# A band mask folded into a one-hot matmul, and the last tile's two stores on one queue, in a two-layer encoder

## The chip, the cores and the metric

One core of one Trainium2 chip runs the whole program. The metric is the device time of one execution in microseconds (us), as the median of several runs; less is better. The core has five engines that run side by side and wait for each other by semaphores: TensorE (PE in the profile; PEld is its weight load), VectorE (DVE), ScalarE (ACT), GpSimd (POOL) and SyncE (SP), which issues nearly all DMA transfers of this kernel.

## The reference

Two encoder layers of 1024 tokens by 1024 features. Layer 0 has windowed attention with a learned sink and a relative-position bias (A), dense attention with rotary positions (B) and cross-attention into a memory (X); layer 1 has differential attention with the same bias (C), and X. The change concerns the bias of A and C:

```python
def rel_bias_lookup(table, rel):            # table: 32 buckets x 6 heads
    return jnp.moveaxis(table[t5_bucket(rel)], -1, 0).astype(jnp.float32)

# A: blocks of 128 queries, each against 384 keys
rel = c - BLOCK - a                          # a: 0..127, c: 0..383
bias = rel_bias_lookup(table, rel)
valid = (jnp.abs(rel) <= WINDOW) & ...       # WINDOW = 128
logits = jnp.where(valid, logits + bias, NEG_INF)
p = softmax(concatenate([logits, sink_col]))[..., :-1]

# C: every query against all 1024 keys, bias added, no band
p = softmax(s + rel_bias_lookup(table, rel))
```

After each layer the output is projected and added to the residual; at the end a last RMSNorm is taken of every row.

## The kernel before

**Work and order.** Activations are kept transposed, features on partitions, as a high and a low float32r part, so that a projection tile (`proj_jobs`, L329) is 24 matmuls of 128x512 for each half of the tokens. Attention goes in steps of 128 queries, and projections ("jobs") are cut into pieces that are pulled between the steps to fill PE. `run_steps` writes out the order by hand: in step i it emits the scores of step i, the transposes of an earlier step, the product with V of a still earlier one, and job pieces between them. Tile then places the instructions on the engines; each engine, and the SP queue of transfers too, works strictly in its own order.

**The bias.** `tab` holds the bias table, negated, because the kernel takes all scores negative. One matmul of `tab` with a one-hot matrix `oh` (32 buckets by 512 relative positions) gives `vp`, one row for each head; it goes over `vs` to `vec_d` in HBM. `skew(h)` writes row h 128 times into `skew_d`, so that `skew_src(h)`, read with a row step of 511, gives a 128x384 tile in which each row is shifted by one against the row above. Layer 1 loads that tile as part of `toep` (`load_toep`). Layer 0 loads it into `ab` (`a_bias`, two buffers, one load for each of the six A heads, while the head before is at work), and POOL then adds `mask`, a 128x384 tile from HBM with 1e30 outside the band (L1152). The scores of an A step, `sa`, are read by DVE's L1184, which adds `ab` and writes `e`.

**The loop around it in layer 0.** A step's scores become exponentials in a tile `e` (three buffers; ACT's L1110 for B, L1188 for A). DVE takes the reciprocal of the row sums (`rz`, L1113 or L1192), POOL multiplies `e` by it (L1114 for B, L1198 for A), SP copies `e` to `er` (`word_copy`, L175), PE transposes `er` (`te`, `ta`). The buffer `e` is free for the third step after it when that copy has landed. POOL also takes the head outputs times the gate (`gy`, L473, from DVE's `yt`, L472) and the low parts of weights (`wl`, L243).

**The tail.** The last of the 16 row tiles is scaled in two parts, 384 columns on ACT (L1349) and 640 on DVE (L1350). Each is stored by a transfer of its own: the 384 columns by ACT's queue (L1352), the 640 by SP's. It is the only transfer that ACT issues.

Of the kernel before, what the change touches and what calls it, by code (L numbers as in the profile page):

```python
# [12 lines left out]
F32 = mybir.dt.float32  # L13
F32R = mybir.dt.float32r
AF = mybir.ActivationFunctionType
ALU = mybir.AluOpType
# [23 lines left out]
XB = 0  # L40
ABLAG = 3
PRE = ((((2, 3, 4, 5), 4), ((6,), 6), ((7,), 6)), (((2, 3), 6), ((4,), 6)))
SPARE = 24
LATE = 22

TILES = (
# [109 lines left out]
def encoder_kernel(ctx, tc, A):  # L156
# [15 lines left out]
    def dma(out, in_, eng=None):  # L172
        if out.dtype == F32R and in_.dtype == F32R:
            out, in_ = out.bitcast(F32), in_.bitcast(F32)
        (eng or nc.sync).dma_start(out=out, in_=in_)  # L175
# [14 lines left out]
    misc = const.tile([P, 8], F32, name="misc")  # L190
    gq, nlam, gs, ls, le = (misc[:, a:b] for a, b in ((0, 1), (1, 2), (2, 3), (3, 5), (5, 7)))
    nsink = const.tile([P, 6], F32, name="nsink")
    tab = const.tile([32, 6], F32, name="tab")
    edge = pool(ctx, "edge", "right").tile([P, 120], F32, name="edge")
    spare = const.tile([P, SPARE], F32, name="spare")
    for t in (spare, edge):
# [12 lines left out]
    memT_d = [dr.tile([P, KT, MEM], F32R, name="memT%d" % i) for i in range(2)]  # L209
    wo_d = [[[dr.tile([P, 8, 512], F32R, name="wo%d%d%s" % (l, nh, c)) for c in "hl"] for nh in range(2)]  # L210
            for l in range(2)]
    vec_d = dr.tile([6, 512], F32, name="vec_d")
    skew_d = dr.tile([6, P, 512], F32, name="skew_d")

    nc.gpsimd.memset(sm.tile([P, 16], F32, tag="pad", name="pad", bufs=1), 0.0)

# [182 lines left out]
    def sg(M, name="sg", dt=F32R):  # L399
        return M.pl.tile([P, 512], dt, tag="sg", name=name, bufs=M.cfg["sg"])  # L400
# [633 lines left out]

    dma(tab, A["rel_bias"])
    nc.vector.tensor_scalar(out=tab, in0=tab, scalar1=-1.0, scalar2=None, op0=ALU.mult)
    oh = sg(M, "oh", F32)[:32, :]
    dma(oh, A["onehot"])  # L1040
    vp = ps_t("vp")
    nc.tensor.matmul(vp[0:6, :], tab, oh, start=True, stop=True)
    vs = sg(M, "vs", F32)[:6, :]
    nc.vector.tensor_copy(vs, vp[0:6, :])
    dma(vec_d, vs)

    def skew(h):
        dma(skew_d[h], bass.AP(vec_d.tensor, vec_d.offset + h * 512, [[0, P], [1, 512]]))
# [15 lines left out]
    def skew_src(h):  # L1064
        return bass.AP(skew_d.tensor, skew_d.offset + h * P * 512 + 127, [[511, P], [1, 384]])
# [74 lines left out]
    def open_ab():  # L1140
        top_stack.close()
        ab = pool(top_stack, "ab", "right")
        mask = ab.tile([P, 384], F32, name="mask")
        dma(mask, A["mask"])
        abias["mask"], abias["pool"] = mask, ab
        M.xpool, M.xbufs = ab, XB

    def a_bias(h):
        mask = abias["mask"]
        t = abias["pool"].tile([P, 384], F32, tag="ab", name="ab", bufs=2)  # L1150
        dma(t, skew_src(h))
        nc.gpsimd.tensor_tensor(out=t, in0=t, in1=mask, op=ALU.add)  # L1152
        abias[h] = t

    if True:
# [96 lines left out]

    def hooks0(i):
        if 2 <= i < 8:
            skew(i - 2)
        if i < 0:
            wout_hook(0, jobs, "g2", r1)

# [6 lines left out]
    def out_proj(l, hT_next, stack, ahead=None):  # L1265
        op = pool(stack, "op%d" % l, "right" if l == 0 else "left")
        gb = bcast_row(op, A["odd_norm"][0] if l == 0 else A["final_norm"], "gb")
        while len(wout) < 16:
            wout[len(wout)] = load_wout(l, len(wout), r1 if l == 0 else r2)
        src = x_d if l == 0 else x1sc  # L1270
        ne = EARLY[l]
        pre = {t: k for ts, k in PRE[l] for t in ts if "pre%d" % t in jobs.done}

        def xres(t):
            xr = op.tile([P, D], F32, tag="xr", name="xr", bufs=2)
            dma(xr, (xpsc[l] if t in pre else src)[t * P:(t + 1) * P, :])
            return xr

        def pieces(i):
            if i == 2:  # L1280
                p = [(ps_a("po")[:, 0:512], c, 512) for c in (0, 512)]
                return p, p
            if i < TT - 1:
                S2 = ps_s("po")
                return [(S2[:, 0:512], 0, 512), (S2[:, 512:1024], 512, 512)], [(S2, 0, 1024)]
            p = [(ps_a("po")[:, 0:512], 0, 512)]
            for c, n in ((512, 512),) if l == 0 else ((512, 256), (768, 256)):
                p.append(((ps_a if c == 512 else ps_t)("po")[:, 0:n], c, n))
            return p, p

        mms = []

        def mm(ps_, ch, ks, first):
            for acc, c, n in ps_:
                for k in ks:
                    for _ in y_mm(acc, ch, c // 512, k, k == first, k == 7, slice(c % 512, c % 512 + n)):
                        mms.append(lastmm[0])

        def turn():
            while pend and len(mms) >= pend[0][2]:  # L1300
                xs, t, d = pend.pop(0)
                transpose_tile(xs, hT_next, t, mms[d - 1])

        def chunk(t):
            return y_chunk(l, t, range(pre.get(t, 0), 8))

        order = ORD[l]
        pend, due = [], [0]
        chs = [chunk(t) for t in order[:2]]
        accs = {}  # L1310
        for i in range(2):
            t = order[i]
            accs[i] = pieces(i)
            mm(accs[i][0], chs[i], range(pre.get(t, 0), ne), pre.get(t, 0))
        xrs = [xres(t) for t in order[:2]]
        for i, t in enumerate(order):
            xr = xrs[i]
            mps, eps = accs[i] if i < 2 else pieces(i)
            mm(mps, chs[i], range(ne if i < 2 else pre.get(t, 0), 8), pre.get(t, 0))
            if i + 2 < TT:  # L1320
                chs.append(chunk(order[i + 2]))
                xrs.append(xres(order[i + 2]))
            turn()
            rows = slice(t * P, (t + 1) * P)
            x1 = op.tile([P, D], F32, tag="x1", name="x1", bufs=2)
            xs = op.tile([P, D], F32, tag="xs", name="xs", bufs=2)
            ss = stat("z4", 4)
            tail = l == 1 and i == TT - 1
            for j, (acc, c, n) in enumerate(eps):
                h = slice(c, c + n)  # L1330
                nc.vector.tensor_tensor(out=x1[:, h], in0=acc, in1=xr[:, h], op=ALU.add)
                nc.scalar.activation((xr if tail or l == 0 else xs)[:, h], x1[:, h], AF.Square,
                                     accum_out=ss[:, j:j + 1])
                if tail:
                    nc.vector.tensor_tensor(out=xs[:, h], in0=x1[:, h], in1=gb[:, h], op=ALU.mult)
                elif l == 0:
                    nc.gpsimd.tensor_tensor(out=xs[:, h], in0=x1[:, h], in1=gb[:, h], op=ALU.mult)
                if l == 0:
                    dma(x1sc[rows, h], x1[:, h])

            v = stat("v")
            nc.vector.tensor_scalar(out=v, in0=ss[:, 0:1], scalar1=1.0 / D, scalar2=EPS, op0=ALU.mult, op1=ALU.add)
            for j in range(1, len(eps)):
                nc.vector.scalar_tensor_tensor(out=v, in0=ss[:, j:j + 1], scalar=1.0 / D, in1=v,
                                               op0=ALU.mult, op1=ALU.add)
            r = stat("r")
            rstd_from(r, v, 1)
            if tail:
                nc.scalar.activation(xs[:, 0:384], xs[:, 0:384], AF.Identity, scale=r)  # L1349
                nc.vector.tensor_scalar(out=xs[:, 384:1024], in0=xs[:, 384:1024], scalar1=r, scalar2=None,  # L1350
                                        op0=ALU.mult)
                nc.scalar.dma_start(out=out_d[rows, 0:384], in_=xs[:, 0:384])  # L1352
                dma(out_d[rows, 384:1024], xs[:, 384:1024])
            elif l == 0:
                nc.scalar.activation(xs, xs, AF.Identity, scale=r)
            else:
                for _, c, n in eps:
                    h = slice(c, c + n)
                    nc.vector.scalar_tensor_tensor(out=xs[:, h], in0=x1[:, h], scalar=r, in1=gb[:, h],
                                                   op0=ALU.mult, op1=ALU.mult)  # L1360
                    dma(out_d[rows, h], xs[:, h])
            if l == 0:
                due[0] = max(len(mms) + LATE, due[0] + 18)
                pend.append((xs, t, due[0]))
        while pend:
            next(ahead)
            mms.extend([lastmm[0]] * 8)
            turn()
# [267 lines left out]
def _constants():  # L1636
# [14 lines left out]
    large = 8 + (np.log(nf / np.float32(8)) / np.float32(math.log(16.0)) * np.float32(8)).astype(np.int32)  # L1651
    large = np.minimum(large, 15)
    b = np.where(rel > 0, 16, 0) + np.where(n < 8, n, large)
    onehot = (np.arange(32)[:, None] == b[None, :]).astype(np.float32)
    r = np.arange(384)[None, :] - 128 - np.arange(128)[:, None]
    mask = np.where(np.abs(r) <= 128, 0.0, 1e30).astype(np.float32)
    return dict(cosT=cosT, sinT=sinT, onehot=onehot, mask=mask)


# [14 lines left out]
```

## Time and profile before

| | |
|---|---|
| median of 3 runs | 1227.74 us (1226.81 to 1227.98) |
| profiled execution, its own time | 1230.69 us |
| its span, first to last instruction | 1228.9 us |
| PE busy | 1196.5 us, 97% of the span |
| DVE, ACT, POOL busy | 65%, 54%, 36% |
| mean granted TensorE clock | 0.996 |

The span is what the trace covers; 1.8 us of the execution's own time lie outside it. Busy shares are means over stages: what an engine's work is worth is read at the place where someone waits for it. In the rows below, a time in brackets is how long the engine sat idle before the row, and behind the arrow is what ended that.

### The profile page before, as it was taken

The page shows a single profiled execution, that of the slowest core. Times are in us where ns is not written, and L with a number is a line of the kernel's source. Part 1 is how long each engine was busy: PE and PEld are TensorE (multiplying, and loading weights), DVE is VectorE, ACT ScalarE, POOL GpSimd, SP SyncE. Part 2 cuts the span into 40 slices and gives each one's busy share as a digit, 9 for nine tenths or more (in the row PEclk, how much of TensorE's full clock was granted, in tenths as well). Part 3 has the DMA queues.
Part 4 walks back from the last instruction along what each step waited for, and adds up shares of the span by engine and source line. Part 5 has one row for each costly group of instructions (what it writes and reads, how often), then busy time and mean ns, then how long its engine had stood idle before and what let it go on. Part 6 is the DMA issues. An engine that isn't in the chain of part 4 may idle for free.

```text
span 1228.9 us, 19560 instructions
## 1 busy us (share of the span) xinstructions
PE 1196.5 (97%) x6614; PEld 988.4 (80%) x6614; DVE 801.1 (65%) x1495; ACT 663.1 (54%) x1477; POOL 436.3 (36%) x414
## 2 busy tenths in 40 slices
PE   6999999999999999999999999999999999999997
PEld 5788888888888777888888777777787777777886
DVE  5547665377778878635365866766767767667544
ACT  6248754366667766636157744555545454445332
POOL 5023365366665455437112222333143231301100
PEclk9999999999999999999999999999999999999999
DMA  6664445545465565457645445355363452468354
GB/s 257 200 194 147 163 172 163 166 160 207 163 233 209 208 227 191 151 196 237 186 158 156 153 146 164 121 183 163 124 187 125 153 171 105 149 212 285 121 192 155
DMA packets 114304, 216.70 MB, mean 176 GB/s; under 512 B 13302, under 2 KB 47478, under 8 KB 114204
## 3 DMA queue, kind: packets, MB, share of 16 engines
q1 hardware_dynamic: 114060, 215.25, 52.5%
q8 instruction: 53, 0.87, 0.3%
q14 instruction: 47, 0.39, 0.1%
q10 hardware_dynamic: 144, 0.20, 0.0%
HBM read 87.71 MB, written 39.86 MB: 104 GB/s over the span
## 4 chain that ended last, share of the span: by engine, by line
PE 47%; DVE 2%; DMA 1%; issue 1%; ACT 1%; POOL 0%; POOLq 0%; SPq 0%; DVEq 0%; ACTq 0%
PE acc L329 24%; PE po L702 5%; PE oc L1545 3%; PE sc L1505 3%; PE te L580 3%; PE sc L1514 2%; PE pre L702 2%; PE oc L1547 2%; DMA wr<-in_w_in 1%; PE ssqc L1563 1%; PE ox L656 0%; PE rbcc L1576 0%; PE tv L439 0%; PE sx L543 0%; DVE e L1520 0%
## 5 line engine op out<-in xcount | busy, mean ns | idle before, releaser
L329 PE MATMUL acc<-h,wh 128*128 128x512 f32 x1536 | 499.5, 398 | 1.6 <-DVE h L351 0.8
L329 PEld LDWEIGHTS acc<-h,wh 128*128 128x128 f32 x1536 | 282.4, 188 | 65.7 <-issue 7.9
L329 PE MATMUL acc<-h,wl 128*128 128x512 f32 x768 | 303.8, 396 | 1.5 <-POOL wl L243 1.2
L243 POOL TENSOR_TENSOR wl<-wr,wh 128x512 fp32r<-128x512 f32 x94 | 124.8, 1329 | 286.3 <-DVE wh L241 155.0
L1523 ACT ACTIVATE e<-e,mn 128x1024 f32<-128x1024 f32 x96 | 110.0, 1148 | 117.0 <-DVE mn L1520 116.9
L329 PEld LDWEIGHTS acc<-h,wl 128*128 128x128 f32 x768 | 144.3, 188 | 34.9 <-issue 4.4
L1114 POOL TENSOR_TENSOR e<-e,rz 128x1024 f32<-128x1024 f32 x48 | 91.6, 1910 | 84.2 <-DVE rz L1113 57.8
L1520 DVE CUSTOM_DVE_ANT_0 e<-sc,toep 128x1024 f32<-128x1024 f32 x96 | 113.5, 1218 | 8.0 <-PE sc L1514 7.3
L580 PEld LDWEIGHTS te<-identr,er 128*128 128x128 f32 x896 | 92.2, 143 | 18.8 <-PE sa L543 2.2
L580 PE MATMUL te<-identr,er 128*128 128x128 f32 x896 | 99.9, 246 | 4.3 <-DVE O L1578 1.4
L348 DVE TENSOR_TENSOR PT<-te,PT 128x512 fp32r<-128x512 f32 x112 | 74.3, 687 | 42.8 <-ACT PT L347 39.2
L241 DVE CAST wh<-wr 128x512 fp32r<-128x512 f32 x112 | 58.2, 522 | 42.9 <-PE acc L329 17.3
L348 DVE TENSOR_TENSOR PTl<-te,PTh 128x512 fp32r<-128x512 f32 x112 | 74.0, 684 | 9.4 <-ACT PTh L347 8.9
L1545 PE MATMUL oc<-PT,v 128*128 128x512 f32 x192 | 69.8, 403 | 0.7 <-DVE ckl L1420 0.7
L1532 DVE SCALAR_TENSOR_TENSOR e<-e,mr 128x1024 f32<-128x1024 f32 x48 | 66.3, 1381 | 1.5
L347 ACT CAST PT<-te 128x512 fp32r<-128x512 f32 x112 | 62.7, 589 | 7.2 <-PE te L580 6.7
L347 ACT CAST PTh<-te 128x512 fp32r<-128x512 f32 x112 | 62.2, 586 | 7.9 <-PE te L580 7.1
L702 PE MATMUL po<-woh,yh 128*128 128x512 f32 (+1 forms) x172 | 65.7, 382 | 0.0
L702 PE MATMUL po<-woh,yl 128*128 128x512 f32 (+1 forms) x172 | 65.5, 381 | 0.0
L702 PE MATMUL po<-wol,yh 128*128 128x512 f32 (+1 forms) x172 | 65.3, 380 | 0.0
L1105 DVE TENSOR_REDUCE mn<-sb 128x1 f32<-128x1024 f32 x48 | 58.3, 1216 | 7.0 <-PE sb L543 6.6
L350 ACT ACTIVATE yh<-yr 128x256 fp32r<-128x256 f32 (+2 forms) x56 | 24.0, 447 | 66.2 <-DMA yr<-ysc 37.5
(211 smaller groups left out, 2358.7 us busy)
## 6 DMA issues: line engine op xcount, KB each, us to landing
er<-e SPq DMA_DIRECT2D x112, 512.0 KB, 3.0
wr<-in_w_in SPq DMA_DIRECT2D x96, 256.0 KB, 3.0
ysc<-gy SPq DMA_DIRECT2D x16, 512.0 KB, 2.7
cq<-sg SPq DMA_DIRECT2D x64, 128.0 KB, 2.5
ck<-sg SPq DMA_DIRECT2D x48, 128.0 KB, 2.3
er<-e SPq DMA_DIRECT2D x12, 384.5 KB, 2.6
xpsc<-xh SPq DMA_DIRECT2D x18, 256.0 KB, 2.6
xr<-xpsc SPq DMA_DIRECT2D x9, 512.0 KB, 3.6
```

The lines of the kernel that those rows point to most:

```text
L243: (nc.vector if fast else nc.gpsimd).tensor_tensor(out=lo, in0=raw, in1=hi, op=ALU.subtract)
L329: lastmm[0] = nc.tensor.matmul(acc, a, b[:, k, c0:c0 + n], start=(i == 0), stop=(i == 23))
L347: nc.scalar.copy(hi, src)
L348: return nc.vector.tensor_tensor(out=lo, in0=src, in1=hi, op=ALU.subtract)
L580: nc.tensor.transpose(to[:, i * P:(i + 1) * P], e[0][:, k * P:(k + 1) * P], idt)
L702: lastmm[0] = nc.tensor.matmul(acc, a, b, start=(start and n == 0), stop=(stop and n == 2))
L1105: nc.vector.tensor_reduce(out=mn, in_=Sp, op=ALU.min, axis=AX.X)
L1114: nc.gpsimd.tensor_tensor(out=et, in0=et, in1=rz.to_broadcast([P, 1024]), op=ALU.mult)
L1520: nc.vector.tensor_tensor_reduce(out=et, in0=Sp, in1=toeps[h][:, w0:w0 + 1024], scale=1.0, scalar=BIG, op0=ALU.add, op1=ALU.min, accum_out ...
L1523: nc.scalar.activation(et, et, AF.Exp, bias=mn[:, m:m + 1], scale=-1.0, accum_out=z[:, m:m + 1])
L1532: nc.vector.scalar_tensor_tensor(out=es[0], in0=es[1], scalar=c, in1=es[0], op0=ALU.mult, op1=ALU.add)
L1545: nc.tensor.matmul(acc, V[:, kt, 0, :], ph.both[:, kt, :], start=(kt == 0), stop=(kt == 7), skip_group_check=True)
```

## The change

Three edits. (1) `tab` gets 33 rows and 12 columns: the table twice, and a 33rd row that is 0 in the first six columns and, after the negation, 1 in the last six. The one-hot matrix gets a 33rd row with the band (0 inside, 1e30 outside) and 12 further columns that hold that row of `tab`. One matmul then gives twelve rows: six without the band (for layer 1) and six with it (for the A heads). (2) `skew` is called twelve times instead of six, `a_bias` reads the rows with the band, and the `mask` tile, its load and POOL's six additions are gone. (3) The last tile's two stores both go to the SP queue.

```diff
-    tab = const.tile([32, 6], F32, name="tab")
+    tab = const.tile([33, 12], F32, name="tab")
...
-    vec_d = dr.tile([6, 512], F32, name="vec_d")
-    skew_d = dr.tile([6, P, 512], F32, name="skew_d")
+    vec_d = dr.tile([12, 512], F32, name="vec_d")
+    skew_d = dr.tile([12, P, 512], F32, name="skew_d")
...
-    dma(tab, A["rel_bias"])
+
+    for i in range(2):
+        dma(tab[:32, 6 * i:6 * i + 6], A["rel_bias"])
+    dma(tab[32:33, :], A["onehot"][32:33, 512:524])
     nc.vector.tensor_scalar(out=tab, in0=tab, scalar1=-1.0, scalar2=None, op0=ALU.mult)
-    oh = sg(M, "oh", F32)[:32, :]
-    dma(oh, A["onehot"])
+    oh = sg(M, "oh", F32)[:33, :]
+    dma(oh, A["onehot"][:, 0:512])
     vp = ps_t("vp")
-    nc.tensor.matmul(vp[0:6, :], tab, oh, start=True, stop=True)
+    nc.tensor.matmul(vp[0:12, :], tab, oh, start=True, stop=True)
...
-        mask = ab.tile([P, 384], F32, name="mask")
-        dma(mask, A["mask"])
-        abias["mask"], abias["pool"] = mask, ab
+        abias["pool"] = ab
...
-        mask = abias["mask"]
         t = abias["pool"].tile([P, 384], F32, tag="ab", name="ab", bufs=2)
-        dma(t, skew_src(h))
-        nc.gpsimd.tensor_tensor(out=t, in0=t, in1=mask, op=ALU.add)
+        dma(t, skew_src(6 + h))
...
         if 2 <= i < 8:
-            skew(i - 2)
+            skew(6 + i - 2)
+        if 10 <= i < 16:
+            skew(i - 10)
...
-                nc.scalar.dma_start(out=out_d[rows, 0:384], in_=xs[:, 0:384])
-                dma(out_d[rows, 384:1024], xs[:, 384:1024])
+                for h in (slice(384, 1024), slice(0, 384)):
+                    dma(out_d[rows, h], xs[:, h])
```

On POOL, this is the place of the last of the six additions, for the sixth A head in the later part of layer 0. Before:

```order
L1198 TENSOR_TENSOR e<-e,rz_5053 128x384
L1198 TENSOR_TENSOR e<-e,rz_5053 128x256
L473 TENSOR_TENSOR gy<-yt,gy 64x256
L1152 TENSOR_TENSOR ab<-ab,mask 128x384
L473 TENSOR_TENSOR gy<-yt,gy 64x256
L1114 TENSOR_TENSOR e<-e,rz 128x1024 x2
L1198 TENSOR_TENSOR e<-e,rz_5237 128x256
L1198 TENSOR_TENSOR e<-e,rz_5237 128x384
```

Now (three lines lie further down in the file, so L1114 is L1117, and L1198 is L1197):

```order
L1197 TENSOR_TENSOR e<-e,rz_5054 128x384
L1197 TENSOR_TENSOR e<-e,rz_5054 128x256
L473 TENSOR_TENSOR gy<-yt,gy 64x256 x2
L1117 TENSOR_TENSOR e<-e,rz 128x1024 x2
L1197 TENSOR_TENSOR e<-e,rz_5238 128x256
L1197 TENSOR_TENSOR e<-e,rz_5238 128x384
```

The addition between the two `gy` products is gone, and nothing else moved; it is the same at the other five places.

On the SP queue, near the start of layer 0, `wr` are weight loads, `er<-e` the copies of the first attention steps. Before:

```order
L175 DMA wr<-in_w_mem 128x512 x2
L175 DMA skew_d<-vec_d 128x512 x5
L175 DMA wr<-in_w_in 128x512 x2
L175 DMA er<-e 128x1024
L175 DMA wr<-in_w_in 128x512 x2
L175 DMA er<-e 128x1024
```

Now:

```order
L175 DMA wr<-in_w_mem 128x512 x2
L175 DMA skew_d<-vec_d 128x512 x5
L175 DMA wr<-in_w_in 128x512 x2
L175 DMA skew_d<-vec_d 128x512 x2
L175 DMA er<-e 128x1024
L175 DMA skew_d<-vec_d 128x512
L175 DMA wr<-in_w_in 128x512
L175 DMA skew_d<-vec_d 128x512 x2
L175 DMA wr<-in_w_in 128x512
L175 DMA skew_d<-vec_d 128x512
L175 DMA er<-e 128x1024
```

The six further `skew` transfers stand here, in the gaps between the first copies and weight loads, although `hooks0` names them eight steps later; behind them the queue is as before, but for the load of `mask`, which is gone.

## Rows read from the trace of the kernel before

**Rows 1.** Busy by window: window, length, PE, PEld, DVE, ACT, POOL, clock, DMA.

```profile
20.00:388.00 368.00, 365.48 (x2136) 311.81 (x2134) 239.89 (x452) 220.71 (x512) 178.90 (x153) 1.00 0.53 179
388.00:573.00 185.00, 176.67 (x1018) 149.57 (x1018) 129.36 (x254) 115.12 (x261) 93.04 (x82) 0.98 0.60 209
```

**Rows 2.** Busy by window, around one stall of PE.

```profile
438.16:440.39 2.23, 0.00 (x1) 0.01 (x1) 0.69 (x3) 0.27 (x2) 1.60 (x3) 1.00 0.75 309
440.39:443.81 3.42, 3.42 (x14) 3.12 (x15) 2.83 (x6) 1.42 (x4) 0.72 (x1) 0.50 0.78 270
```

**Rows 3.** Timeline before that stall, PE and DVE: start, length, engine, line.

```profile
431.09 0.43 DVE L472 TENSOR_TENSOR yt<-oa,yt 64x256 f32<-64x256 f32 x1
...
432.15 0.15 DVE L1113 RECIPROCAL rz<-z 128x1 f32<-128x1 f32 x1
...
437.77 0.39 PE L543 MATMUL sb<-bkl,q 128*128 128x512 f32 x1
...
439.70 0.62 DVE L1184 CUSTOM_DVE_ANT_0 e<-sa,ab,nsink 128x384 f32<-128x384 f32 x1 [3.04 <-DMA er<-e]
...
440.39 0.69 PE L543 MATMUL sa<-ak,q 128*128 128x384 f32 x1 [2.23 <-DVE mn L1184]
```

**Rows 4.** Timeline of POOL before that stall.

```profile
432.21 1.56 POOL L1152 TENSOR_TENSOR ab<-ab,mask 128x384 f32<-128x384 f32 x1 [3.79 <-DMA ab<-skew_d]
433.85 0.73 POOL L473 TENSOR_TENSOR gy<-yt,gy 64x256 f32<-64x256 f32 x1
434.67 3.75 POOL L1114 TENSOR_TENSOR e<-e,rz 128x1024 f32<-128x1024 f32 x2
```

**Rows 5.** Timeline of the SP queue there, and landings of `er` (425 to 441 us).

```profile
432.90 0.81 SPq L175 DMA_DIRECT2D xh<-in_x  x2
436.59 2.32 SPq L175 DMA_DIRECT2D er<-e  x2
...
DMA to landing us min/median/max: 2.6/2.9/2.9
```

**Rows 6.** The tile `ab` over the whole run: uses, durations in ns, landings.

```profile
L1152 POOL TENSOR_TENSOR ab<-ab,mask x6: 1008/1017/1564, 218.7 to 432.2; 128x384 f32<-128x384 f32 x6
...
DMA to landing us min/median/max: 2.7/3.5/3.8
```

**Rows 7.** Timeline of PE at the next long wait.

```profile
464.77 0.39 PE L543 MATMUL sa<-ak,q 128*128 128x256 f32 x1 [1.07 <-DVE mn L1184]
```

**Rows 8.** The tile `tab`: its load and use; landing.

```profile
L175 SPq DMA_DIRECT2D tab<-in_rel_bias x1: 429/429/429, 22.6 to 22.6; - x1
L1038 DVE TENSOR_SCALAR tab<-tab x1: 150/150/150, 32.8 to 32.8; 32x6 f32<-32x6 f32 x1
...
DMA to landing us min/median/max: 5.0/5.0/5.0
```

**Rows 9.** Timeline of PE just behind the one-hot matmul.

```profile
55.85 0.73 PE L329 MATMUL acc<-h,wh 128*128 128x512 f32 x2 [0.25 <-DVE gy L460]
```

**Rows 10.** The `skew` transfers, the first copy and its transposes; busy in between.

```profile
70.55 3.06 SPq L175 DMA_DIRECT2D skew_d<-vec_d  x5
...
77.20 0.50 SPq L175 DMA_DIRECT2D er<-e  x1
...
90.77 0.80 PE L580 MATMUL te<-identr,er 128*128 128x128 f32 x8
...
76.00:80.00 4.00, 4.00 (x23) 3.47 (x22) 1.99 (x3) 2.15 (x8) 0.00 (x0) 1.00 0.99 364
```

**Rows 11.** The last two stores: issues, and us from issue to landing.

```profile
1224.88 0.33 SPq L175 DMA_DIRECT2D out<-xs  x1
1224.95 0.38 ACTq L1352 DMA_DIRECT2D out<-xs  x1
...
out<-xs SPq DMA_DIRECT2D x1, 320.0 KB, 2.6
out<-xs ACTq DMA_DIRECT2D x1, 192.0 KB, 3.0
```

More of the change, by code (lines that the diff above doesn't have):

```diff
@@ L42 @@
 PRE = ((((2, 3, 4, 5), 4), ((6,), 6), ((7,), 6)), (((2, 3), 6), ((4,), 6)))
-SPARE = 24
+SPARE = 16
 LATE = 22
@@ L1033, in encoder_kernel @@
             dma(memT_d[i][:, 4 * j:4 * j + 4, :], memT[i].tiles[j])
-    dma(tab, A["rel_bias"])
+    for i in range(2):
+        dma(tab[:32, 6 * i:6 * i + 6], A["rel_bias"])
+    dma(tab[32:33, :], A["onehot"][32:33, 512:524])
     nc.vector.tensor_scalar(out=tab, in0=tab, scalar1=-1.0, scalar2=None, op0=ALU.mult)
-    oh = sg(M, "oh", F32)[:32, :]
-    dma(oh, A["onehot"])
+    oh = sg(M, "oh", F32)[:33, :]
+    dma(oh, A["onehot"][:, 0:512])
     vp = ps_t("vp")
-    nc.tensor.matmul(vp[0:6, :], tab, oh, start=True, stop=True)
-    vs = sg(M, "vs", F32)[:6, :]
-    nc.vector.tensor_copy(vs, vp[0:6, :])
+    nc.tensor.matmul(vp[0:12, :], tab, oh, start=True, stop=True)
+    vs = sg(M, "vs", F32)[:12, :]
+    nc.vector.tensor_copy(vs, vp[0:12, :])
     dma(vec_d, vs)
@@ L1653, in _constants @@
     b = np.where(rel > 0, 16, 0) + np.where(n < 8, n, large)
[L1654 to L1657, printed above, removed]
+    onehot = np.zeros((33, 524), np.float32)
+    onehot[:32, :512] = np.arange(32)[:, None] == b[None, :]
+    onehot[32, :512] = np.where(n <= 128, 0.0, 1e30)
+    onehot[32, 518:] = -1
+    return dict(cosT=cosT, sinT=sinT, onehot=onehot)
 def kernel(**inputs):
```

## The prediction, made before the changed kernel was run

> **What bounds the kernel now.** I read the page first: PE is busy 97% of the span, so a microsecond is won only where PE waits or runs slowly, and work taken from POOL (36%) or from transfers counts only if PE waits for it. Next I cut the run into windows [rows 1]. From 20 to 388 us PE is busy 365.48 of 368.00 us at full clock: nothing to win there. From 388 to 573 us, the later part of layer 0, it is busy 176.67 of 185.00 us, and the mean clock is 0.98: this is where PE waits, and where the clock falls. Then I listed PE's waits in that stretch. The longest of the whole run behind the start is 2.23 us before 440.39 us [rows 2]: PE does nothing from 438.16 to 440.39, and the next 3.42 us run at a granted clock of 0.50, the lower of the two levels (1.2 GHz instead of 2.4).
>
> Last I followed this wait back, engine by engine. PE's `sa` at 440.39 follows DVE's L1184, which ran from 439.70 to 440.32, after 3.04 us in which DVE had nothing else and waited for a copy `er<-e` to free the buffer `e` [rows 3]. That copy is the first of the two that SP issued from 436.59 on [rows 5]; 2.9 us to land brings it to 439.5. SP's issue waited for POOL's product L1114, the first of two from 434.67 on (half of 3.75 us, so until 436.55) [rows 4]. And POOL came to it late: it sat 3.79 us idle until the load of `ab` landed, added the mask from 432.21 to 433.77 (1.56 us, the longest of the six), took `gy` from 433.85 to 434.58, and only then had its turn at `e`. The inputs of both had been ready long before: `yt` at 431.52, `rz` at 432.30 [rows 3]. So POOL stood in its own order before an addition whose result nobody needed yet, and PE waited 6 us later.
>
> **The change, part by part.**
>
> **The six additions go.** Five of them lie before 388 us, where PE does not wait; I cost their loss at nothing, and PE's queue of projection matmuls is what hides them now. For the sixth the order on POOL is `gy`, `e`, `e` without the addition. `gy` can start at 431.55 and ends at 432.28; `e` starts when `rz` is there, at 432.33 instead of 434.67, that is 2.34 us sooner. SP is free by 433.71 (two loads from 432.90, 0.81 us [rows 5]), so the copy goes out at 434.25 instead of 436.59, and everything behind moves with it: L1184 ends at 440.32 - 2.34 = 437.98. PE is through with `sb`, its work before the wait, at 438.16. The wait of 2.23 us is gone, by 0.2 us. What can be late in its place: the copy now runs beside the two loads issued at 432.90. The trace has no `er` copy there; the landings of `er` near by are 2.6 to 2.9 us, of `ab`, a smaller load that met other traffic, 2.7 to 3.8 us [rows 6]. So the copy is 0 to 0.9 us later than I count; less the 0.2 us of slack, PE would wait 0 to 0.7 us. I take 0.2, near the `er` rows: -2.0 us, bounds -2.2 and -1.5.
>
> **The clock.** The 3.42 us behind the wait run at half clock with PE always busy [rows 2]. At full clock they take half, 1.71 us. If PE doesn't stop, I see nothing that lowers the clock there: -1.7 us, bounds -1.7 and 0. The Trainium skill, "TensorE: Matmul & The Clock Gate", section "Part 1: The HAM clock gate", says that the gate looks at activity in windows that run freely, so that the same idle gap may or may not lower the clock, by where it falls. By that rule the drop is no sure consequence of this gap, and in an execution where it does not happen anyway the sum would end 1.7 us smaller; the trace shows one execution only, in which the drop follows the gap at once.
>
> **Where the gain could stay behind.** From 440 to 464 us PE has no wait over 0.3 us, and the other engines follow its matmuls, so I let the gain pass through. I take nothing off here; the next long wait, 1.07 us before 464.77 [rows 7], is a rival below.
>
> **The mask's load goes** from SP's queue at 209 us, in the stretch without waits: nothing.
>
> **DVE's L1184 waits for the load of `ab` itself** instead of for POOL. The load is issued while the head before is at work; the sixth landed at about 432.2, where POOL's wait ended, and its first use is the L1184 above, 437.3 at the soonest: covered by 5 us.
>
> **`tab` with three loads.** The one load is issued at 22.6 and lands 5.0 us later, at 27.6; DVE uses `tab` at 32.8 [rows 8]. Two further issues of 0.43 us bring the last landing to 28.5. Cover 4.3 us; without it DVE, which then prepares PE's first operands, would hold PE by the excess. Nothing.
>
> **The matmul with 33 rows and 12 columns.** Its columns streamed are still 512, so I take the same time. Its load `oh` has one row more. Behind it PE waits 0.25 us for `gy` on DVE anyway [rows 9]; a delay up to that is free, and beyond it PE waits too. Bounds 0 and +0.5 us, and I take 0, since one row in 33 is 3% of a small load.
>
> **Six more `skew` transfers.** Five took 3.06 us of SP's time, 0.61 each, and in the window they fill, 76 to 80 us, the 16 transfer engines are busy at 0.99 and move 364 GB/s [rows 10]; a `skew` writes 128 x 512 x 4 bytes = 0.26 MB, so an estimate from that row is 0.72 us each, 4.3 us for six. Behind them stand the first copy `er<-e` (issued 77.20) and weight loads. The copy's transposes run at 90.77: 77.20 + 2.9 + 4.3 = 84.4, so 6 us are left. Nothing; if that cover were gone, PE would wait by the excess.
>
> **The tail.** SP issues the 640 columns at 1224.88 (landing 2.6 us later, 1227.48), ACT the 384 at 1224.95 (landing after 3.0, 1227.95) [rows 11]; the later one ends the run. On one queue the second issue follows 0.40 us behind the first (half of 0.81 [rows 5]), at 1225.28, and lands 2.6 to 3.0 us later, 1227.88 to 1228.28. Against 1227.95 that is -0.1 to +0.3; I take +0.1. The Trainium skill, "DMA: Bandwidth & Descriptors", section "Issuing engines are not separate DMA queues", says that issuing from two engines saves only the issue time. By it this edit only costs, about one issue (0.33 us) at most, and wins nothing; the rows leave room for a small gain too, because ACT's smaller transfer landed later after its issue than SP's larger one.
>
> **Sum.** -2.0 - 1.7 + 0.1 = -3.6 us. The profiled execution took 1230.69 us, 2.95 more than the median; made against it the sum gives 1227.1 us, and the same difference on the median 1227.74 gives 1224.1 us.
>
> **The rivals.** A change under 0.2%, 2.5 us, is about what a measurement of this kernel cannot tell from none.
>
> *Only the wait goes, the clock's part stays.* The drop of the clock may be absent in timed executions, which are faster than the profiled one, or a wait left over may still bring it. Then -2.0 + 0.1 = -1.9 us: 1225.8 us.
>
> *The gain is given back at the next wait.* PE reaches 464.77 earlier, but if DVE, with its own backlog, is not earlier, the wait there grows from 1.07 towards 4.7 us. For it: DVE is busy 129 of 185 us in this stretch [rows 1], and L1184 is the same instruction that PE waited for at 440. Against it: DVE's own 3.04 us of idleness go with the same copy. Given back in full this is +0.1 us; with a new drop of the clock for 1.7 us, +1.8 us. Some 1227 to 1229 us, mostly no measurable change.
>
> *Slower: the first attention steps starve.* The six `skew` transfers fill SP's queue and the transfer engines ahead of the first copies and weight loads. It begins to cost when the copy issued at 77.20 lands after 90.77, 6 us later than I count, for instance if a `skew` took 1.7 us of the engines instead of 0.72. It decides when it costs over the 3.6 us won and 2.5 us more, 6.1 us of waiting, or 4.4 us with a clock drop of 1.7: then 1230.2 us and more. Against it: five such transfers in a row made no wait over 0.7 us before.
>
> *More than counted.* POOL earlier also shortens later waits of the stretch, 8.3 us in all [rows 1]: 1222 to 1223 us.
>
> **How the numbers follow.** The forecast (wait and clock) 0.50, the wait alone 0.22, given back 0.15, starving 0.07, more than counted 0.06. The forecast's 1224.1 us is my number; its own bounds are 1223.4 to 1225.2. The range of all: from 1222.8, where the last case is cut in part, to 1227.6, where most of "given back" is in; left out are about 0.17. Faster by over 0.2% means under 1225.28: nearly all of the forecast, the last case, a little of the wait alone, 0.56. Within 0.2%: the rest of those and most of "given back", 0.37. Slower: 0.07.
>
> **What would show it.** Right: no addition on POOL; its `gy`, `e`, `e` near 432 without a gap; copies at about 434.3; no wait of PE near 438; no clock of 0.50 there; PE's busy time from 388 on unchanged in a stretch 3.6 us shorter. Wrong: a wait of PE at the same place behind another copy, a longer one at 464, a wait near 60 to 100 us, or a last landing over 0.4 us later after the last scaling. Most likely to break it is that a wait that PE no longer makes at 438 turns up at a later step.

## The result and the profile after

| | before | changed |
|---|---|---|
| median of 22 runs each | 1227.63 us (1224.36 to 1230.93) | 1229.12 us (1226.46 to 1233.40) |
| ratio, run against run | | 1.0020, 95% interval 1.0011 to 1.0028 |
| profiled execution, its own time | 1230.69 us | 1230.05 us |
| its span | 1228.9 us | 1228.2 us |

The medians differ by 1.5 us; compared run against run, the changed kernel is slower by 0.20%, some 2.5 us (1.4 to 3.4), where 3.6 us less were forecast. The two profiled executions alone would say the opposite: the changed kernel's span is 0.7 us shorter. That is the first thing to explain, and the windows show where to look. Busy by window of the changed kernel, for the stretches of [rows 1]:

```profile
20.00:388.00 368.00, 363.51 (x2123) 310.62 (x2122) 235.54 (x447) 217.77 (x504) 172.67 (x147) 1.00 0.54 181
388.00:573.00 185.00, 178.19 (x1036) 149.96 (x1035) 133.05 (x259) 118.60 (x268) 93.74 (x81) 1.00 0.62 215
```

PE is busy 1.5 us more of the second stretch, where the gain was forecast, and 2 us less of the first, where I had seen "nothing to win" and not asked what there was to lose. PE's waits in the changed kernel (releaser, total, times, longest) name the place:

```profile
PE ssq L833 <- DVE PTl L348: 2.7, 1, 2.7
PE sa L543 <- DVE mn L1183: 2.2, 3, 1.1
PE ob L1130 <- ACT PTh L347: 1.1, 1, 1.1
```

**The loss, at 94 us.** The wait of 2.7 us is new (0.22 us before). Timeline of the changed kernel, followed back: SP's queue, then DVE, ACT and PE.

```profile
75.61 1.11 SPq L175 DMA_DIRECT2D skew_d<-vec_d  x2
76.82 0.54 SPq L175 DMA_DIRECT2D er<-e  x1
77.41 0.60 SPq L175 DMA_DIRECT2D skew_d<-vec_d  x1
81.04 0.33 SPq L175 DMA_DIRECT2D wr<-in_w_in  x1
81.42 1.11 SPq L175 DMA_DIRECT2D skew_d<-vec_d  x2
82.76 0.40 SPq L175 DMA_DIRECT2D wr<-in_w_in  x1
...
84.61 0.43 DVE L241 CAST wh<-wr 128x512 fp32r<-128x512 f32 x1 [2.13 <-DMA wr<-in_w_in]
88.69 0.43 DVE L241 CAST wh<-wr 128x512 fp32r<-128x512 f32 x1 [3.65 <-DMA wr<-in_w_in]
89.37 1.21 DVE L627 TENSOR_REDUCE mn<-sx 128x4 f32<-128x1024 f32 x1
90.62 0.47 ACT L632 ACTIVATE e<-sx,mn 128x256 f32<-128x256 f32 x1 [5.47 <-DVE mn L627]
90.34 0.80 PE L580 MATMUL te<-identr,er 128*128 128x128 f32 x8
97.16 1.05 PE L833 MATMUL ssq<-small,sq 128*128 128x2 f32 x8 [2.70 <-DVE PTl L348]
117.90 1.05 PE L833 MATMUL ssq<-small,sq 128*128 128x2 f32 x8 [0.30 <-ACT sq L820]
```

The same places in the kernel before:

```profile
81.80 2.04 SPq L175 DMA_DIRECT2D wr<-in_w_in  x2
84.44 0.43 DVE L241 CAST wh<-wr 128x512 fp32r<-128x512 f32 x1 [1.52 <-DMA wr<-in_w_in]
86.54 0.43 DVE L241 CAST wh<-wr 128x512 fp32r<-128x512 f32 x1 [1.68 <-DMA wr<-in_w_in]
88.58 0.48 ACT L632 ACTIVATE e<-sx,mn 128x256 f32<-128x256 f32 x1 [2.99 <-DVE mn L627]
95.12 1.05 PE L833 MATMUL ssq<-small,sq 128*128 128x2 f32 x8 [0.22 <-DVE PTl L348]
114.72 1.05 PE L833 MATMUL ssq<-small,sq 128*128 128x2 f32 x8 [0.30 <-ACT sq L820]
```

The second weight load is issued no later than before (82.76 us, where the pair of before is issued from 81.80 to 83.84), but it lands 5.8 us after its issue (2.9 at most in the kernel before), and DVE's cast follows at 88.69 instead of 86.54. DVE, which works in its order, stands before the cast of that weight, and behind the cast wait `mn`, ACT's exponentials, ACT's `sq` and DVE's `PTl`, which PE needs. PE has no slack there: it waited 0.22 us for the same `PTl` before the change. From the transposes `te` to the second `ssq` it takes 117.90 - 90.34 = 27.56 us, before it 114.72 - 90.77 = 23.95 [rows 10]: 3.6 us lost, 2.5 of them waiting, the rest at half clock (0.83 mean in 94 to 104 us). Why the load lands late stands in the windows, first of the changed kernel, then of before (last columns: clock, busy share of the transfer engines, GB/s):

```profile
80.00:84.00 4.00, 4.00 (x31) 3.80 (x30) 1.36 (x3) 2.86 (x9) 2.32 (x2) 1.00 1.00 336
84.00:88.00 4.00, 4.00 (x24) 3.37 (x23) 0.43 (x1) 0.60 (x2) 1.29 (x1) 1.00 0.95 257
```

```profile
80.00:84.00 4.00, 4.00 (x31) 3.77 (x30) 2.02 (x4) 3.14 (x10) 2.58 (x2) 1.00 0.29 106
84.00:88.00 4.00, 4.00 (x25) 3.42 (x24) 1.87 (x4) 0.75 (x2) 2.19 (x2) 1.00 0.70 234
```

The six `skew` transfers fill the engines for 8 us in which they had been half free (busy 0.29 and 0.70). The Trainium skill, "DMA: Bandwidth & Descriptors", section "Queues, rings and completion order", says that a transfer is split over rings of its queue and that each transfer engine takes the descriptors of a ring in order, though a later one may finish first. From that it follows that a load starts behind what its queue issued before it, and the trace agrees: the issue took 0.40 us, the landing 5.8. Whether a load on another queue would have been as late, since all share the same busy engines, no run here tests.

**The gain, at 438 us.** In the changed kernel POOL and SP do what was forecast:

```profile
422.59 0.38 PE L1130 MATMUL ob<-PTh,v 128*128 128x256 f32 x1 [1.09 <-ACT PTh L347]
433.51 0.74 POOL L473 TENSOR_TENSOR gy<-yt,gy 64x256 f32<-64x256 f32 x1 [3.24 <-DVE yt L472]
434.39 4.01 POOL L1117 TENSOR_TENSOR e<-e,rz 128x1024 f32<-128x1024 f32 x2
436.58 2.32 SPq L175 DMA_DIRECT2D er<-e  x2
440.01 0.62 DVE L1183 CUSTOM_DVE_ANT_0 e<-sa,ab,nsink 128x384 f32<-128x384 f32 x1 [1.47 <-POOL e L1197]
440.68 0.44 PE L543 MATMUL sa<-ak,q 128*128 128x384 f32 x1 [0.67 <-DVE mn L1183]
```

POOL no longer waits for a load between its two `gy`. To compare, take off the 2.79 us by which the changed kernel is late at `ob` (422.59; 419.80 in the kernel before): the copies go out at 433.79 (forecast 434.25), and L1184, now L1183, starts at 437.22 (forecast 439.70 - 2.34 = 437.36). Yet 0.67 us of waiting are left, because PE was ready at 440.01 - 2.79 = 437.22 and not at 438.16 as in [rows 2]. Here is the row that explains it, PE of the kernel before, and the window around it:

```profile
419.80 0.50 PE L1127 MATMUL ob<-PTh,v 128*128 128x256 f32 x1 [1.41 <-ACT PTh L347]
...
416.00:425.00 9.00, 7.59 (x40) 6.37 (x40) 6.68 (x14) 5.93 (x16) 3.76 (x3) 0.81 0.59 199
```

The profiled execution of before had run at half clock behind `ob` already (0.81 mean in these 9 us). The second trace of the kernel before, below, runs there at full clock and shows what the half clock changed: it slowed PE's way to 438 us, made the chain behind POOL late by more, and so set the size of the stall that I priced.

**The tail.** Last scaling and stores of the changed kernel:

```profile
1223.60 0.55 DVE L1351 TENSOR_SCALAR xs<-xs,r 128x640 f32<-128x640 f32 x1 [0.73 <-POOL r L231]
1224.18 0.81 SPq L175 DMA_DIRECT2D out<-xs  x2
```

The scaling in the kernel before:

```profile
1224.30 0.55 DVE L1350 TENSOR_SCALAR xs<-xs,r 128x640 f32<-128x640 f32 x1 [0.73 <-POOL r L231]
```

From the start of the scaling to the end of the span it takes 1228.2 - 1223.60 = 4.6 us; before, 1228.9 - 1224.30 = 4.6. These two traces show neither a cost nor a gain.

### The profile page after: what moved, and what is told of

It reads as the page before. It is cut to its first block, busy times and chain, and to the rows that moved or that the text cites. A ratio compares the mean times of both kernels' runs of the same rounds, so it can differ in the third digit from the quotient of the medians.

```text
span 1228.2 us, 19567 instructions
## 1 busy us (share of the span) xinstructions
PE 1194.5 (97%) x6614; PEld 986.7 (80%) x6614; DVE 800.0 (65%) x1495; ACT 663.6 (54%) x1477; POOL 430.3 (35%) x408
## 4 chain that ended last, share of the span: by engine, by line
PE 57%; DVE 4%; DMA 2%; issue 2%; ACT 2%; SPq 0%; POOL 0%; POOLq 0%; DVEq 0%; ACTq 0%
PE acc L329 23%; PE po L702 9%; PE pre L702 5%; PE te L580 3%; PE oc L1546 3%; PE sc L1506 3%; PE sc L1515 2%; PE oc L1548 2%; DMA wr<-in_w_in 1%; PE ob L1130 1%; DMA wr<-in_w_mem 1%; PE sb L543 1%; PE oa L1235 1%; PE tx L377 1%; PE ssqc L1564 1%
## 5 line engine op out<-in xcount | busy, mean ns | idle before, releaser
L1117 POOL TENSOR_TENSOR e<-e,rz 128x1024 f32<-128x1024 f32 x48 | 92.0, 1918 | 90.8 <-DVE rz L1116 57.9
```

The lines of the kernel that those rows point to most:

```text
L1117: nc.gpsimd.tensor_tensor(out=et, in0=et, in1=rz.to_broadcast([P, 1024]), op=ALU.mult)
```

## The experiments

Theory A: the six further `skew` transfers delay a weight load and cost about 3.6 us. Theory C: the half-clock stretches at 420 and 440 us belong to one execution, and without them POOL's addition is worth about 1 us, not 3.6. The rivals, B and D, are in the expectations. Two groups of four kernels were timed; ratios are against the kernel before in the same group.

| run | median us (runs) | ratio, 95% interval | PE's wait near 97 us |
|---|---|---|---|
| hold_skews | 1226.20 (12) | 0.9998, 0.9988 to 1.0007 | 0.23 |
| before_skews | 1231.54 (6) | 1.0043, 1.0028 to 1.0058 | 3.50 |
| half_skews | 1224.57 (12) | 0.9988, 0.9973 to 1.0004 | 0.44 |
| before_again | 1226.81 (12) | 1.0007, 0.9994 to 1.0019 | 0.23 |
| kernel before, first group | 1226.40 (29) | | |
| after_again | 1229.03 (12) | 1.0026, 1.0017 to 1.0036 | 2.77 |
| hold_again | 1225.03 (12) | 0.9994, 0.9985 to 1.0003 | 0.22 |
| late_add | 1224.81 (11) | 0.9994, 0.9985 to 1.0004 | 0.33 |
| tail_only | 1226.35 (12) | 1.0003, 0.9992 to 1.0013 | 0.60 |
| kernel before, second group | 1225.59 (35) | | |

### hold_skews and hold_again: the further transfers held to later steps

In the changed kernel nothing keeps the six transfers to the steps that `hooks0` names, since the row they read is ready early; the scheduler puts them where the queue has room. An order edge behind the transfer traced last keeps them there:

```diff
-        (eng or nc.sync).dma_start(out=out, in_=in_)
+        lastdma[0] = (eng or nc.sync).dma_start(out=out, in_=in_)
...
         if 10 <= i < 16:
-            skew(i - 10)
+            with tc.issue_after(lastdma[0].ins): skew(i - 10)
```

> The changed kernel with its six further skew transfers held at the attention steps that hooks0 names: each is queued behind the transfer traced last, one per step from about 105 to 190 us, instead of at 75 to 84 us. Nothing else moves on any engine. Theory A (the six transfers fill the transfer engines, the weight load issued at 82.76 us lands 5.8 us later, DVE stands before its cast and PE loses 2.5 us near 94 us, and about 1.1 us more at half clock): the wait of 2.70 us near 97 us goes back to about 0.2, no granted clock under 1.00 at 94 to 104 us, and the time falls 2.5 to 3.6 us under the changed kernel: 1225 to 1227 us, 1 to 2.5 us under the kernel before. Rival B (the loss near 97 us is chance, and the time comes from elsewhere, for instance the 33-row matmul or the tail): the wait may go, but the time stays within 1 us of the changed kernel, 1228 to 1230 us.

> The same kernel as hold_skews, for a second trace and a narrower interval. If the mask's edit is worth what the stall of 1.23 us in the second trace of the kernel before allows (a wait shorter by 0.4 to 0.7 us and no clock to regain in most executions), the ratio is 0.999 to 1.000; if it is worth the forecast's 3.6 us, or 2.0 for the wait alone, 0.997 to 0.9985. No wait over 0.5 us at 94 to 98 us, and about 0.6 to 0.9 us before the third step of the sixth A head at 437 us.

PE of hold_skews, near 97 us and at the old stall:

```profile
94.99 1.05 PE L833 MATMUL ssq<-small,sq 128*128 128x2 f32 x8 [0.23 <-DVE PTl L348]
...
437.92 0.44 PE L543 MATMUL sa<-ak,q 128*128 128x384 f32 x1 [0.84 <-DVE mn L1183]
```

The wait is gone with the place of six transfers alone, and so is the loss: in the second group 1225.03 us against 1229.03 for the changed kernel. Theory A holds, rival B falls. The rest of the change, now without that cost, measures -0.2 us in one group (0.9998) and -0.7 in the other (0.9994); neither is clear of zero. The intervals end at -1.5 and -1.8 us: they exclude the forecast's 3.6 us and, narrowly, the 1.9 of "only the wait goes" too. My expectation for hold_skews, 1 to 2.5 us under before, was still too high; hold_again came out as expected (0.9994, waits of 0.22 and 0.76 us).

### before_skews: the transfers alone, in the kernel before

```diff
-    skew_d = dr.tile([6, P, 512], F32, name="skew_d")
+    skew_d = dr.tile([12, P, 512], F32, name="skew_d")
...
-    def skew(h):
-        dma(skew_d[h], bass.AP(vec_d.tensor, vec_d.offset + h * 512, [[0, P], [1, 512]]))
+    def skew(h, d=0):
+        dma(skew_d[h + d], bass.AP(vec_d.tensor, vec_d.offset + h * 512, [[0, P], [1, 512]]))
...
         if 2 <= i < 8:
             skew(i - 2)
+        if 10 <= i < 16:
+            skew(i - 10, 6)
```

> The kernel before with the six further skew transfers alone, at the same places of SP's queue as in the changed kernel (a second copy of the six rows, which nobody reads); POOL's six additions, the mask and the stores as before. Theory A: a wait of 2.3 to 2.8 us before 97 us and half clock behind it; 2.5 to 3.6 us slower than before, 1230 to 1231 us; with the stall at 438 us still there. Rival B: within 1 us of the kernel before.

DVE's cast and PE's wait in before_skews, and the window:

```profile
90.26 0.43 DVE L241 CAST wh<-wr 128x512 fp32r<-128x512 f32 x1 [4.02 <-DMA wr<-in_w_in]
...
98.73 1.87 PE L833 MATMUL ssq<-small,sq 128*128 128x2 f32 x8 [3.50 <-DVE PTl L348]
...
94.00:104.00 10.00, 6.50 (x25) 5.31 (x24) 5.00 (x9) 6.38 (x16) 3.03 (x2) 0.68 0.14 58
```

The transfers alone make the kernel before 0.43% slower, 5.3 us (3.4 to 7.1): the same mechanism, with a longer wait and more half clock (0.68 mean against 0.83) than in the changed kernel. From `te` (91.09) to the second `ssq` (120.50) its trace takes 29.41 us, 5.5 more than before, where the changed kernel's takes 3.6 more. The size was over my 2.5 to 3.6; the wait was too (3.50 against 2.8 at most). Why the same transfers cost more here is not shown.

### half_skews: the same issues, half the bytes

```diff
         if 10 <= i < 16:
-            skew(i - 10)
+            with tc.issue_after(lastdma[0].ins): skew(i - 10, 64, 64)
+            skew(i - 10, 0, 64)
```

(`skew(h, a, n)` writes n rows from row a on, and `lastdma` is as in hold_skews.)

> The changed kernel with the six further skew transfers cut in two: rows 0 to 63 at 75 to 84 us as now, rows 64 to 127 one per step from about 105 us on. The same number of issues stands ahead of the weight load, with half the bytes. If the bytes are the cause (transfer engines 1.00 busy at 80 to 84 us): six times 0.13 MB at the 364 GB/s of rows 10 are an estimated 2.2 us instead of 4.3, the weight load lands about 3.7 instead of 5.8 us after its issue, and PE waits 0.2 to 0.7 us instead of 2.70 near 97 us: 1225.5 to 1227.5 us. If the number of issues on SP's queue is the cause: the wait stays at 2.3 to 2.7 us, and the time at 1228 to 1230 us.

Half_skews: window, DVE's cast, PE's wait; the last line is of the tile `wr` from 80 to 92 us, from issue to landing.

```profile
80.00:84.00 4.00, 4.00 (x31) 3.80 (x30) 1.40 (x4) 2.86 (x9) 2.29 (x2) 1.00 0.61 196
...
86.39 0.43 DVE L241 CAST wh<-wr 128x512 fp32r<-128x512 f32 x1 [1.99 <-DMA wr<-in_w_in]
...
94.87 1.05 PE L833 MATMUL ssq<-small,sq 128*128 128x2 f32 x8 [0.44 <-DVE PTl L348]
...
DMA to landing us min/median/max: 2.5/2.8/3.5
```

In the changed kernel the last of these lines reads 2.6/3.4/5.8. With as many issues ahead of the load and half the bytes, it lands in 3.5 us at most and PE waits 0.44: the bytes (and with them the number of rows written) are the cause, not the places in SP's queue. The time, 1224.57 us, is under the 1225.5 to 1227.5 that I expected.

### before_again and after_again: second traces

> The kernel before, unchanged, for a second trace and more runs. Theory C (the two stretches at half clock at 420 and 440 us, 1.7 us each, are not in every execution; the profiled one was 2.95 us over the median for that): this trace shows at most one of them, and its own time is then 1.7 or 3.4 us under 1230.69. Rival D (they are in every execution, and the 2.95 us lie elsewhere): granted clock of 0.50 behind both waits again. Either way the ratio to the kernel before is 1.000 within 0.001, which is the floor of this measurement.

> The changed kernel, unchanged, for a second trace. If the wait near 97 us belongs to the six further skew transfers, it is there again, 2.3 to 3.5 us long behind a weight load that lands 5 us or more after its issue; if it was chance, it is under 1 us. In time 2 to 3.5 us above the kernel before.

Before_again: POOL's addition, PE at `ob` and at the stall, and the two windows.

```profile
429.43 1.01 POOL L1152 TENSOR_TENSOR ab<-ab,mask 128x384 f32<-128x384 f32 x1 [3.59 <-DMA ab<-skew_d]
...
418.57 0.38 PE L1127 MATMUL ob<-PTh,v 128*128 128x256 f32 x1 [1.36 <-ACT PTh L347]
437.39 0.45 PE L543 MATMUL sa<-ak,q 128*128 128x384 f32 x1 [1.23 <-DVE mn L1184]
...
416.00:425.00 9.00, 7.64 (x50) 6.48 (x50) 8.03 (x18) 6.87 (x17) 4.27 (x4) 1.00 0.74 253
437.00:446.00 9.00, 8.61 (x53) 7.24 (x54) 8.08 (x17) 6.75 (x15) 4.83 (x5) 1.00 0.66 249
```

Both stretches are at full clock here, and the stall is 1.23 us. PE is ready 17.59 us behind `ob` (18.36 in the first trace), and POOL comes to its `e` 13.09 us behind it, at 431.66 (14.87 in the first): in the first trace the chain is 1.8 us later and PE 0.8, which makes the 1.0 us by which its stall is longer. So the half-clock stretches are not in every execution, as theory C says. Its size was off: this execution took 1224.53 us, 6.2 less than the first profiled one, and not 1.7 or 3.4. Some 1.2 us of that were lost ahead of `ob`, 1.8 between `ob` and the stalled `sa`, and the remaining 3.2 behind it, of which the second half-clock stretch is 1.7. After_again shows the new wait again (2.77 us, a load that lands 5.6 us after its issue): it is no chance.

### late_add: the additions kept, POOL's wait for the load removed

```diff
                 if p == 1 and h < 5:
                     a_bias(h + 1)
+                if p == 2 and h < 5:
+                    a_mask(h + 1)
...
-        nc.gpsimd.tensor_tensor(out=t, in0=t, in1=mask, op=ALU.add)
         abias[h] = t
...
+    def a_mask(h):
+        t, mask = abias[h], abias["mask"]
+        with (tc.issue_after(lastp[0].ins) if h else nullcontext()):
+            nc.gpsimd.tensor_tensor(out=t, in0=t, in1=mask, op=ALU.add)
```

(`lastp` is POOL's last product `e`; head 0's addition follows its load as before.)

> The kernel before with its six additions of the mask, but each queued on POOL one A step later, behind that engine's last product e: POOL does the same work and no longer sits idle before the load of ab. No further skew transfers, stores as before. If POOL's wait for that load (3.79 us in the first trace, 3.59 in the second) is what makes PE wait near 437 us, the wait there falls from 1.23 us to 0.6 to 0.9 us, as without the additions, and the time is 0.4 to 1 us under before: ratio 0.999 to 1.000. If the addition's own 1.0 to 1.6 us on POOL are the cause, they only move and the wait turns up behind them, with the time unchanged or longer.

POOL and PE of late_add:

```profile
431.10 0.74 POOL L473 TENSOR_TENSOR gy<-yt,gy 64x256 f32<-64x256 f32 x1 [3.24 <-DVE yt L472]
431.99 4.02 POOL L1115 TENSOR_TENSOR e<-e,rz 128x1024 f32<-128x1024 f32 x2
...
438.33 0.45 PE L543 MATMUL sa<-ak,q 128*128 128x384 f32 x1 [0.72 <-DVE mn L1192]
...
449.23 1.02 POOL L1159 TENSOR_TENSOR ab<-ab,mask 128x384 f32<-128x384 f32 x1
```

Near 438 us POOL looks as if the addition were gone; it stands at 449.23, without a wait, and PE's wait is 0.72 us. So it was the place of the addition in POOL's order, ahead of products that were ready, and not its existence. As far as these intervals tell, an order edge gives what the mask's edit gives (0.9994 both), without a matmul row or a transfer more.

### tail_only: both stores on SP's queue

The diff is the last one of the change.

> The kernel before with the last tile's two stores both on SP's queue, 640 columns first; nothing else. The prediction's +0.1 us (-0.1 to +0.3): from the start of the last scaling to the end of the span 4.3 to 4.7 us, as before (4.6 and 4.4 in the two traces of before); ratio 1.000 within the interval. The rival rule that only an issue is lost: +0.3 us, 4.8 us or more from the scaling to the end.

The scaling starts at 1220.02 and the span ends at 1224.5: 4.5 us. Over all traces it is 4.6, 4.4, 4.7 and 4.2 with the store on ACT's queue (before, before_again, before_skews, late_add) and 4.6, 4.7, 4.3, 4.3, 4.3 and 4.5 with both on SP's (changed, after_again, hold_skews, hold_again, half_skews, tail_only). No difference shows. By the Trainium skill's rule that the prediction weighed ("DMA: Bandwidth & Descriptors", section "Issuing engines are not separate DMA queues") up to 0.3 us could have been lost; the traces do not show that either.

## Why the prediction was wrong, point by point

All ten traces at the stall, PE's idle times before `ob` and before the third `sa` of the fifth A head (the addition ahead of it is for the sixth), and the distance between the two (us):

| trace | addition ahead of `gy` | idle before `ob` | clock behind it | idle before `sa` | `ob` to `sa` |
|---|---|---|---|---|---|
| before | yes | 1.41 | 0.50 | 2.23 | 20.59 |
| before_again | yes | 1.36 | 1.00 | 1.23 | 18.82 |
| tail_only | yes | 1.25 | 1.00 | 1.23 | 18.76 |
| before_skews | yes | 1.11 | 1.00 | 1.22 | 19.49 |
| changed | no | 1.09 | 1.00 | 0.67 | 18.09 |
| after_again | no | 1.17 | 1.00 | 0.69 | 18.03 |
| hold_skews | no | 1.10 | 1.00 | 0.84 | 18.21 |
| hold_again | no | 1.09 | 1.00 | 0.76 | 17.58 |
| half_skews | no | 1.22 | 1.00 | 0.59 | 17.73 |
| late_add | moved | 1.30 | 1.00 | 0.72 | 17.88 |

- **"The six additions go: -2.0 us."** Right mechanism, size off. POOL, the copies and DVE came forward as worked out. But "PE is through with `sb` at 438.16" was a time with a half-clock stretch ahead of it. Without one the wait is 1.23 us and falls to 0.59 to 0.84: 0.4 to 0.6 us. From `ob` to `sa` the mean of the three traces with the addition at full clock is 19.0 us, that of the six without it there 17.9: 1.1 us in all. No timed run shows that 1.1 us clear of noise.
- **"The clock: -1.7 us."** Failed. Of the ten traces only the first has half clock at 420 or 440 us, so in the median there was next to nothing to win. The sign stood in my own sum: the profiled execution took 2.95 us more than the median, and I carried the difference along as a constant instead of asking which rows it was made of. Two stretches of 3.42 us at half clock cost 3.4 us. Of the 29 runs of before in the first group, 17 have a mean clock of 0.999 (1225.7 us on average) and 4 have 0.996, that of the profiled one (1229.6 us); of the 35 in the second group none has it.
- **"Six more `skew` transfers: nothing."** Failed, and it decides the sign. The price of the bytes was about right (4.3 us estimated; from 80 to 88 us the engines are busy for 3.8 us more than before). The cover was read at the wrong victim: I followed the copy issued at 77.20, which has 6 us to spare, and named the weight loads in the same queue without asking who waits for them. The trace of before showed DVE idle 1.52 and 1.68 us for just these loads, so they had no cover, and the term of 0 measured +3.6 us in the trace. The wait came where the prediction had put a sign of being wrong, "near 60 to 100 us". The rival "the first attention steps starve" was this mechanism at another instruction, priced at 1230.2 us and more with 0.07; the 3.6 us it had to eat up were 1.1.
- **"The tail: +0.1 us."** Within its bounds; the traces show no difference.
- **`tab`, `oh`, the matmul, the mask's load: nothing.** Right. The matmul takes 586 ns (584 before), and PE's wait behind it is 0.39 us (0.25).
- **"L1184 above" as the first use of the sixth `ab`** was wrong, without consequence: that L1184 still belongs to the head before, so the load has more cover than I counted.

Read in the traces, the two parts fit the whole: +3.6 us near 97 us and -1.1 near 438 make +2.5; the ratios give +2.5 us (1.4 to 3.4) and +3.2 (2.1 to 4.4). The timed parts fit less closely: the transfers alone cost 5.3 us, and the rest of the change gains 0.2 and 0.7. That the profiled spans say -0.7 comes from the first trace of before: its distance from `ob` to `sa` is 1.6 us over the mean of the other three with the addition, and another half-clock stretch follows. The second traces have spans of 1222.7 (before) and 1227.3 us (changed), 4.6 more.

One place is in neither part. In the changed kernel another weight load, issued at 927.31, lands late, DVE stands before its cast again, and PE waits for DVE's `O`:

```profile
931.99 0.43 DVE L241 CAST wh<-wr 128x512 fp32r<-128x512 f32 x1 [2.81 <-DMA wr<-in_w_in]
938.95 0.54 PE L580 MATMUL te<-identr,er 128*128 128x128 f32 x4 [1.59 <-DVE O L1579]
```

DVE's wait there is 2.68 us in after_again, 2.65 in before, 2.43 in before_skews and 1.86 in before_again, and 0.77 to 1.13 in the other five traces; PE's is 1.54, 1.42, 1.22, 0.66 and none. So part of the difference between the changed kernel and the held one may lie here. No run settles why that load is late in some traces.

What also stays open: whether one of the three quicker variants (hold_skews, late_add, half_skews) is faster than before; all lie clear under the changed kernel (0.9988 to 0.9998 against its 1.0020 and 1.0026), but all their intervals against before hold 1.000. Nor is it settled why the clock fell in the first trace of before and not in the others.

## What to carry to other kernels

Before a stall is priced from one execution, compare that execution's own time with the median: where it is longer by about what the stall is to give back, take a second trace. Transfers that are added can cost whoever waits for a load behind them, so list every load issued in the same stretch and look for an engine that already sits idle for one: it has no cover. And where an instruction waits in an engine's order ahead of work that is ready, try moving it before removing it: here the move took as much off the wait (0.72 us left, against 0.59 to 0.84) and needed no further transfer.

## What the runs showed of the hardware

Idle gaps of PE of nearly the same length had different ends: behind 1.41 us the clock fell to 0.50 in one trace, behind 1.36, 1.30, 1.25 and 1.23 us it stayed at 1.00 in others, and behind 2.70, 2.77 and 3.50 us it fell in each. The length of one gap does not decide it: in tail_only the clock was 0.50 from 20 to 23 us behind two gaps of 0.99 and 0.57 us, and in before_again it stayed at 1.00 at the same place behind 1.63 and 0.56. The Trainium skill, "TensorE: Matmul & The Clock Gate", section "Part 1: The HAM clock gate", says that its windows run freely; from that it follows that one gap may end either way, and the traces agree. The prediction cites that rule, and its case deserved more than the 0.22 that I gave it.
